# Rotary embedding over 16 heads: one input load in two parts, on two queues

## The chip, the cores and the metric

The kernel runs on one core of one Trainium2 chip. The metric is device time in microseconds, as the median of several runs of the whole program. A core has five instruction streams: TensorE (PE), VectorE (DVE), ScalarE (ACT), GpSimd (POOL) and SyncE (SP). Each runs its own instructions in order and waits on semaphores that the others, or finished transfers, count up. Transfers between HBM and the core's own memory (128 partitions) are done by 16 DMA engines; ScalarE and SyncE each have a queue on which they issue them.

## The reference

The input x has 16 batches of 512 rows of 1024 floats, seen as 16 heads of 64. Each head's two halves are rotated by tables of cosines and sines with one entry per row and half position.

```python
x = x.reshape(batch, seq, num_heads, head_dim)
x1, x2 = x[..., :half_dim], x[..., half_dim:]
cos = cos[None, :, None, :]
sin = sin[None, :, None, :]
rotated = np.concatenate([x1 * cos - x2 * sin, x1 * sin + x2 * cos], axis=-1)
```

Input and output are 33.55 MB each; the tables are 64 KB each.

## The kernel before

**Tiles.** The input is cut into 10 tiles: batches 0 and 1 alone, batches 2 to 13 in six pairs, batches 14 and 15 alone. In a single batch each partition holds 4 consecutive rows of x (16 KB), in a pair 8 rows (32 KB). So a single is a transfer of 2048 KB and a pair one of 4096 KB, and each is one DMA over 128 partitions. Tile 3, the second pair, is batches 4 and 5. The compute engines work on "rows": one row is 128 partitions by 1024 values, four of them in a single and eight in a pair, 64 rows (`u` from 0 to 63) in all. Tile 3 is rows 16 to 23.

**Memory.** `x_sb` is a ring of 40 rows, so it holds ten batches, tiles 0 to 5. The result of a row is written in place, and the tile is stored from there. Tiles 6 to 9 go into places that an earlier tile leaves, and can only be loaded when that one's store has landed.

**One row.** POOL (line 257) multiplies the row with its halves swapped by the sine table and writes `t2_sb` (6 buffers). VectorE (line 293) multiplies the row by the cosine table and writes `t1_ps` (3 buffers). The sum of the two is made in one of two ways: VectorE adds them (line 304), or, for three of eight rows in the middle (`PE2`), TensorE adds `t2` onto `t1` by a matmul with the identity (line 224) and ScalarE copies the sum out (line 191). One row of eight in each pair (`V2`) has its sine product done by VectorE too (line 286), not by POOL. `wait_added(eng, u)` waits until all rows up to u have been summed.

**Queues.** Loads are issued by ScalarE, stores by SyncE. `on_scalar` first issues the loads of tiles 0 to 5 in order (lines 166 to 168), with the two tables behind tile 0 (line 174). Later tiles are loaded from within its loop over rows (lines 188 to 195): at rows 17, 25 and 33 it waits for the landing of the stores that free the place (line 194) and issues tile 6, tile 7, and tiles 8 and 9. The wait of row 17 is for both single tiles' stores, those of rows 25 and 33 are for the stores of tiles 2 and 3. What ScalarE has to copy after that row stands behind this wait. `on_sync` (line 155) goes through the tiles in order, waits until all rows of a tile are summed and issues its store; the first one waits for rows 0 to 3.

**Landing.** Each tile has one semaphore `sem_in[t]`, counted up by 16 when its load has landed. POOL (line 255) and VectorE (line 279) wait for it at the first row of a tile.

Of the kernel before, what the change touches and what calls it, by code (L numbers as in the profile page):

```python
# [6 lines left out]
def bass_split_heads_rope_kernel(  # L7
# [20 lines left out]
    P = 128  # L28
    R1 = seq // P
# [38 lines left out]
    with ExitStack() as stack:  # L68
# [11 lines left out]
        sem_in = [stack.enter_context(nc.semaphore(f"in{t}")) for t in range(NT)]  # L80
# [20 lines left out]
        def c_of(t, r):  # L101
            return c1_ps[:, r, :] if tiles[t][1] == R1 else pair_ps[:, r // R1, 0, r % R1, :]

        def s_of(t, r):
            return s1_sb[:, r] if tiles[t][1] == R1 else s2_sb[:, r]

        x1 = x.rearrange("b (s r) d -> b s (r d)", r=R1)
        o1 = out.rearrange("b (s r) h d -> b s (r h d)", r=R1)
        x2 = x.rearrange("b s d -> (b s) d").rearrange("(g p r) d -> g p (r d)", p=P, r=R2)
# [3 lines left out]
        def in_dram(single, pairs, t):  # L113
            b, n = tiles[t]
            return single[b] if n == R1 else pairs[b // 2]

        def in_sbuf(t):
            b, n = tiles[t]
            k = b * R1 % RING
            return x_sb[:, k:k + n].rearrange("p n h t d -> p (n h t d)")  # L120

        def where(u):
            t, r = rows[u]
            return t, r, u % RING

        def swapped(k):
            return x_sb[:, k, :, ::-1, :]

        def over_heads(table):
            return table[:, None, :, :].broadcast_to([P, H, 2, HALF])  # L130

        def wait_added(eng, u):

            if n_pe[u]:
                eng.wait_ge(sem_a, n_pe[u])
            if n_comb[u]:
                eng.wait_ge(sem_v, n_comb[u])

        def wait_t2_free(eng, u):

            if u >= NT2:
                v = u - NT2
                if PE2[v]:
                    eng.wait_ge(sem_e, n_pe[v])
                else:
                    eng.wait_ge(sem_v, n_comb[v])

        def stores_of(k):

            return sum(b * R1 // R2 == k for b, _ in tiles)  # L150

        def load(eng, t):
            eng.dma_start(in_sbuf(t), in_dram(x1, x2, t)).then_inc(sem_in[t], 16)  # L153

        def on_sync(sp):
            for u in range(NU):
                t, r, k = where(u)
                if r == tiles[t][1] - 1:
                    wait_added(sp, u)
                    k = u // R2  # L160
                    sp.dma_start(in_dram(o1, o2, t), in_sbuf(t)).then_inc(sem_out[k] if k < EARLY else sem_rest, 16)
            sp.wait_ge(sem_rest, 16 * sum(stores_of(k) for k in range(EARLY, NU // R2)))

        def on_scalar(ae):
            later = {}
            for t, (b, n) in enumerate(tiles):
                if b * R1 + n <= RING:
                    load(ae, t)
                else:

                    later.setdefault((b * R1 - RING) // R2 * R2 + R2 - 1 + LAG, []).append(t)
                if t == 0:
                    for i, (table, sem) in enumerate(((cos, sem_cos), (sin, sem_sin))):
                        ae.dma_start(stage[:, i, :], table.rearrange("(s r) d -> s (r d)", r=R1)).then_inc(sem, 16)  # L174
# [13 lines left out]
            for u in range(NU):  # L188
                if PE2[u]:
                    ae.wait_ge(sem_e, n_pe[u])  # L190
                    ae.activation(xs[:, u % RING, :], t1_ps[:, u % NT1, :], COPY).then_inc(sem_a, 1)  # L191
                for t in later.get(u, ()):
                    k = (tiles[t][0] * R1 - RING) // R2
                    ae.wait_ge(sem_out[k], 16 * stores_of(k))
                    load(ae, t)
# [38 lines left out]
        def on_gpsimd(pl):  # L234
            pl.memset(ident[:], 1.0).then_inc(sem_i, 1)  # L235
            pl.wait_ge(sem_i, 1)
            pl.affine_select(  # L237
                out=ident[:],
                in_=ident[:],
                compare_op=mybir.AluOpType.is_equal,  # L240
                fill=0.0,
                base=0,
                pattern=[[-1, P]],
                channel_multiplier=1,
            ).then_inc(sem_i, 1)
            for u in range(NU):
                if V2[u]:
                    continue
                t, r, k = where(u)
                if (t, r) == (0, 0):  # L250
                    pl.wait_ge(sem_s, 1)
                if (t, r) == (2, 0):
                    pl.wait_ge(sem_s, 2)
                if r == 0:
                    pl.wait_ge(sem_in[t], 16)
                wait_t2_free(pl, u)
                pl.tensor_tensor(  # L257
                    t2_sb[:, u % NT2, :, :, :], swapped(k), over_heads(s_of(t, r)), mult
                ).then_inc(sem_p, 1)

        def on_vector(ve):
            ve.memset(zero[:], 0.0).then_inc(sem_z, 1)  # L262
            ve.wait_ge(sem_cos, 16)
            ve.tensor_copy(c1_ps, stage[:, 0, :].rearrange("s (r d) -> s r d", d=HALF)).then_inc(sem_c, 1)  # L264
            ve.wait_ge(sem_c, 1)
            ve.wait_ge(sem_w, NT1 * EH)

            def pair_tables():
                ve.wait_ge(sem_s, 2)
                row = pair_ps[:, V_ROW // R1, 1, V_ROW % R1, :]  # L270
                ve.tensor_scalar_mul(v_ps[:, 0, :], row, -1.0).then_inc(sem_c, 1)
                ve.tensor_copy(v_ps[:, 1, :], row).then_inc(sem_c, 1)

            first_v = V2.index(True)

            def mul(u):
                t, r, k = where(u)
                if r == 0:
                    ve.wait_ge(sem_in[t], 16)
                if (t, r) == (2, 0):  # L280
                    pair_tables()
                if u == first_v:
                    ve.wait_ge(sem_c, 3)
                if V2[u]:
                    wait_t2_free(ve, u)
                    ve.tensor_tensor(t2_sb[:, u % NT2, :, :, :], swapped(k), over_heads(v_ps), mult)  # L286
                if u >= NT1:
                    v = u - NT1
                    if PE2[v]:
                        ve.wait_ge(sem_a, n_pe[v])  # L290
                    else:
                        ve.wait_ge(sem_v, n_comb[v])
                ve.tensor_tensor(  # L293
                    t1_ps[:, u % NT1, :].rearrange("p (h d) -> p h d", d=HALF),
                    x_sb[:, k, :, :, :].rearrange("p h t d -> p (h t) d"),
                    c_of(t, r)[:, None, :].broadcast_to([P, 2 * H, HALF]),
                    mult,
                ).then_inc(sem_m, 1)

            def comb(u):  # L300
                t, r, k = where(u)
                ve.wait_ge(sem_m, u + 1)
                ve.wait_ge(sem_p, n_pool[u])  # L303
                ve.tensor_tensor(  # L304
                    xs[:, k, :],
                    t1_ps[:, u % NT1, :],
                    t2_sb[:, u % NT2, :, :, :].rearrange("p h t d -> p (h t d)"),
                    add,
                ).then_inc(sem_v, 1)

            for u in range(NU + LEAD):
                if u < NU:
                    mul(u)
                if u >= LEAD and not PE2[u - LEAD]:
                    comb(u - LEAD)

        on_sync(nc.sync)
        on_scalar(nc.scalar)
        on_gpsimd(nc.gpsimd)
        on_tensor(nc.tensor)  # L320
        on_vector(nc.vector)
# [33 lines left out]
```

## Time and profile before

| what | us |
|---|---|
| median of 3 timed runs (161.26 to 161.79) | 161.39 |
| span of the profiled execution, first to last instruction | 160.0 |
| POOL busy, 64 instructions | 134.9 |
| VectorE busy, 117 instructions | 130.1 |
| TensorE matmul busy | 73.7 |
| ScalarE busy | 24.4 |

The profile's times are those of one execution; "span" runs from its first instruction to its last, and the timed runs have some more around it. A group of instructions is named by its line in the kernel, engine and operation, with what it writes and reads. The transfers of the input issued from line 153, in order of issue:

| tile | issued at | lands after | landed at |
|---|---|---|---|
| 0 | 0.81 | 7.8 | 8.6 |
| 1 | 2.18 | 11.7 | 13.9 |
| 2 | 2.96 | 20.6 | 23.6 |
| 3 | 3.45 | 35.0 | 38.5 |
| 4 | 3.95 | 49.0 | 53.0 |
| 5 | 4.48 | 68.1 | 72.6 |
| 6 | 53.77 | 38.2 | 92.0 |
| 7 | 73.26 | 38.0 | 111.3 |
| 8 | 92.80 | 33.0 | 125.8 |
| 9 | 93.17 | 47.2 | 140.4 |

The stores of line 161:

| tile | issued at | lands after | landed at |
|---|---|---|---|
| 0 | 20.25 | 18.8 | 39.1 |
| 1 | 30.80 | 22.9 | 53.7 |
| 2 | 46.81 | 26.4 | 73.2 |
| 3 | 63.46 | 29.3 | 92.8 |
| 4 | 80.85 | 30.9 | 111.8 |
| 5 | 102.36 | 24.2 | 126.6 |
| 6 | 118.77 | 21.8 | 140.6 |
| 7 | 135.10 | 15.1 | 150.2 |
| 8 | 144.03 | 11.1 | 155.1 |
| 9 | 151.14 | 8.8 | 159.9 |

### The profile page before, as it was taken

What the parts mean: (1) busy time and instruction counts of PE and PEld (TensorE: products, weight loads), DVE (VectorE), ACT (ScalarE), POOL (GpSimd) and SP (SyncE); (2) the same over time, 40 slices, a digit from 0 to 9 for tenths busy, and PEclk for the clock granted to TensorE, in tenths of its full rate; (3) what the DMA queues carried; (4) which work ended last, traced back from release to release, by engine and by line L of the source; (5) the groups of instructions that cost most, each with busy time, mean ns of one, the idle gap of its engine ahead of it and who ended that gap; (6) DMA issues with size and microseconds to landing.
All of it is one profiled execution on the core that took longest, in us unless ns stands there. A gap on an engine that the chain in (4) does not pass through costs nothing.

```text
span 160.0 us, 522 instructions
## 1 busy us (share of the span) xinstructions
PE 73.7 (46%) x94; PEld 23.7 (15%) x94; DVE 130.1 (81%) x117; ACT 24.4 (15%) x27; POOL 134.9 (84%) x64
## 2 busy tenths in 40 slices
PE   6050005476427735690948606459439841970000
PEld 1020002021102220220222002002202210320000
DVE  0069998699999998997989709899999989989600
ACT  0420000205020502022022020220220122050000
POOL 1059999999999999999999999698999999289400
PEclk9999999969955865567555685855855599577555
DMA  5999999999999999999999999999999999999997
GB/s 160 401 451 463 401 430 418 410 483 406 401 463 406 494 401 401 483 426 401 467 426 418 410 467 434 401 467 393 420 463 446 418 414 418 479 410 434 414 414 303
DMA packets 3170, 67.26 MB, mean 420 GB/s; under 512 B 352, under 2 KB 608, under 8 KB 608
## 3 DMA queue, kind: packets, MB, share of 16 engines
q10 hardware_dynamic: 1728, 33.69, 49.7%
q1 hardware_dynamic: 1440, 33.56, 48.8%
q14 instruction: 2, 0.02, 0.0%
HBM read 33.69 MB, written 33.55 MB: 420 GB/s over the span
## 4 chain that ended last, share of the span: by engine, by line
DMA 59%; POOL 22%; PE 5%; DVE 3%; issue 2%; ACTq 1%; ACT 1%; DVEq 0%
DMA x_sb<-in_x_dram 41%; POOL t_sb L257 22%; DMA out_dram<-x_sb 18%; PE t_ps L224 5%; DVE x_sb L304 2%; DVE t_ps L293 1%; ACT x_sb L191 1%; ACTq L153 1%; ACTq L174 1%; DVEq L303 0%
## 5 line engine op out<-in xcount | busy, mean ns | idle before, releaser
L257 POOL TENSOR_TENSOR t_sb<-x_sb,s_sb 128x1024 f32<-128x1024 f32 x58 | 134.2, 2358 | 14.2 <-ACT s_sb L183 8.2
L224 PE MATMUL t_ps<-t_sb,ident 128*128 128x512 f32 x84 | 68.9, 973 | 62.8 <-DVE t_ps L293 37.9
L293 DVE TENSOR_TENSOR t_ps<-x_sb,pair_ps 128x1024 f32<-128x1024 f32 x48 | 57.7, 1223 | 9.7 <-ACT x_sb L191 9.7
L304 DVE TENSOR_TENSOR x_sb<-t_ps,t_sb 128x1024 f32<-128x1024 f32 x43 | 52.4, 1218 | 2.1 <-POOL t_sb L257 2.1
L191 ACT ACTIVATE x_sb<-t_ps 128x1024 f32<-128x1024 f32 x21 | 21.5, 1024 | 110.6 <-PE t_ps L224 98.9
L224 PEld LDWEIGHTS t_ps<-t_sb,ident 128*128 128x128 f32 x84 | 21.8, 286 | 109.6 <-DVE t_ps L293 70.0
L293 DVE TENSOR_TENSOR t_ps<-x_sb,tab_ps 128x1024 f32<-128x1024 f32 x16 | 19.3, 1222 | 0.5 <-ACT x_sb L191 0.5
L286 DVE TENSOR_TENSOR t_sb<-x_sb,tab_ps 128x1024 f32<-128x1024 f32 x6 | 7.3, 1212 | 0.0
L264 DVE COPY tab_ps<-stage 128x128 f32<-128x128 f32 x1 | 0.3, 295 | 7.7 <-DMA stage<-in_cos_dram 7.7
L208 PE MATMUL pair_ps<-stage,pick 128*128 128x256 f32 x4 | 2.0, 667 | 5.1 <-DMA stage<-in_sin_dram 5.1
L201 PE MATMUL t_ps<-zero 128*128 128x512 bf16 x6 | 2.7, 630 | 1.3 <-DVE zero L262 1.3
L208 PEld LDWEIGHTS pair_ps<-stage,pick 128*128 128x128 f32 x4 | 1.2, 324 | 6.2 <-issue 6.0
L177 ACT ACT_TABLE_LOAD x1 | 1.3, 1283 | 5.0 <-issue 5.0
L201 PEld LDWEIGHTS t_ps<-zero 128*128 128x128 bf16 x6 | 0.7, 138 | 2.3 <-DVE zero L262 1.2
L262 DVE MEMSET zero<- 128x256 uint32 x1 | 0.3, 272 | 0.9 <-PEq L337 0.9
L182 ACT ACTIVATE s_sb<-stage 128x128 f32<-128x128 f32 x1 | 0.3, 310 | 2.3 <-DMA stage<-in_sin_dram 2.3
L186 ACT ACTIVATE s_sb<-pair_ps 128x256 f32<-128x256 f32 x1 | 0.4, 384 | 1.7 <-PE pair_ps L208 1.7
L235 POOL MEMSET ident<- 128x128 f32 x1 | 0.2, 205 | 0.3 <-POOLq L337 0.3
L177 ACT ACTIVATE pick<-ident 128x256 f32<-128x256 f32 x1 | 0.4, 430 | 0.0
L187 ACT ACTIVATE s_sb<-pair_ps 128x256 f32<-128x256 f32 x1 | 0.4, 377 | 0.0
L237 POOL TENSOR_SCALAR_AFFINE_SELECT ident<-ident 128x128 f32<-128x128 f32 x1 | 0.3, 294 | 0.1
L337 POOL MEMSET const-float32-0.0<- 128x1 f32 x1 | 0.1, 99 | 0.3 <-issue 0.3
(6 smaller groups left out, 1.0 us busy)
## 6 DMA issues: line engine op xcount, KB each, us to landing
x_sb<-in_x_dram ACTq DMA_DIRECT2D x6, 4096.0 KB, 38.1
out_dram<-x_sb SPq DMA_DIRECT2D x6, 4096.0 KB, 25.3
x_sb<-in_x_dram ACTq DMA_DIRECT2D x4, 2048.0 KB, 22.4
out_dram<-x_sb SPq DMA_DIRECT2D x4, 2048.0 KB, 14.9
stage<-in_cos_dram ACTq DMA_DIRECT2D x1, 64.0 KB, 7.6
stage<-in_sin_dram ACTq DMA_DIRECT2D x1, 64.0 KB, 7.3
```

The lines of the kernel that those rows point to most:

```text
L153: eng.dma_start(in_sbuf(t), in_dram(x1, x2, t)).then_inc(sem_in[t], 16)
L174: ae.dma_start(stage[:, i, :], table.rearrange("(s r) d -> s (r d)", r=R1)).then_inc(sem, 16)
L177: ae.activation(pick[:], ident[:].rearrange("q (s k) -> q k s", k=2)[:, :, None, :].broadcast_to([P, 2, 2, P // 2]), COPY).then_inc(sem_g, 1)
L186: ae.activation(s2[:, :, :, 0, :], pair_ps[:, :, 1, :, :], COPY, scale=-1.0)
L191: ae.activation(xs[:, u % RING, :], t1_ps[:, u % NT1, :], COPY).then_inc(sem_a, 1)
L201: pe.matmul(t1_ps[:, k, b * BANK:(b + 1) * BANK], zero[:, 0:P], zero[:], start=True, stop=True).then_inc(sem_w, 1)
L208: pe.matmul(pair_ps[:, k].rearrange("p c r d -> p (c r d)"), pick[:, k].rearrange("q b s -> q (b s)"), stage[:].rearrange("q c f -> q (c f)"),
L224: ins = pe.matmul(t1_ps[:, u % NT1, b * BANK:(b + 1) * BANK], ident[:], t2[:, b * BANK:(b + 1) * BANK], start=False, stop=True, skip_group ...
L257: pl.tensor_tensor(t2_sb[:, u % NT2, :, :, :], swapped(k), over_heads(s_of(t, r)), mult).then_inc(sem_p, 1)
L286: ve.tensor_tensor(t2_sb[:, u % NT2, :, :, :], swapped(k), over_heads(v_ps), mult)
L293: ve.tensor_tensor(t1_ps[:, u % NT1, :].rearrange("p (h d) -> p h d", d=HALF), x_sb[:, k, :, :, :].rearrange("p h t d -> p (h t) d"), c_of ...
L304: ve.tensor_tensor(xs[:, k, :], t1_ps[:, u % NT1, :], t2_sb[:, u % NT2, :, :, :].rearrange("p h t d -> p (h t d)"), add,).then_inc(sem_v, 1)
```

## The change

Tile 3 is loaded by two DMAs instead of one. ScalarE issues, at the same place in its order as before, the part for partitions 0 to 95 (3072 KB). SyncE issues the part for partitions 96 to 127 (1024 KB) at the start of its work: it waits until rows 0 to 2 are summed, issues that part, and then goes on to the first store, which waits for rows 0 to 3 as before. Both parts count up the semaphore of tile 3, which is waited for at 32 instead of 16. All other loads, all stores and all compute instructions are as they were.

```diff
-        def load(eng, t):
-            eng.dma_start(in_sbuf(t), in_dram(x1, x2, t)).then_inc(sem_in[t], 16)
+
+        SHARED = 3
+        PART = P // 4
+
+        def load(eng, t, some=None):
+            if some is None:
+                some = slice(0, P - PART) if t == SHARED else slice(0, P)
+            eng.dma_start(in_sbuf(t)[some, :], in_dram(x1, x2, t)[some, :]).then_inc(sem_in[t], 16)
+
+        def wait_landed(eng, t):
+            eng.wait_ge(sem_in[t], 32 if t == SHARED else 16)
 
         def on_sync(sp):
+            wait_added(sp, R1 - 2)
+            load(sp, SHARED, slice(P - PART, P))
             for u in range(NU):
...
                 if r == 0:
-                    pl.wait_ge(sem_in[t], 16)
+                    wait_landed(pl, t)
...
                 if r == 0:
-                    ve.wait_ge(sem_in[t], 16)
+                    wait_landed(ve, t)
```

## The prediction

> **What bounds the kernel now.** The first view is the page's row of the DMA's busy share over 40 slices, with the queues below it (q10 carries what ScalarE's queue issues, all loads; q1 what SyncE's queue issues, all stores).
>
> ```profile
> span 160.0 us, 522 instructions
> DMA  5999999999999999999999999999999999999997
> q10 hardware_dynamic: 1728, 33.69, 49.7%
> q1 hardware_dynamic: 1440, 33.56, 48.8%
> HBM read 33.69 MB, written 33.55 MB: 420 GB/s over the span
> ```
>
> The reader is to see that the 16 DMA engines are busy in every slice but the first and the last: 49.7 + 48.8 = 98.5% of 160.0 us, 157.6 us. 67.25 MB at the 432 GB/s of the stretch from 111 to 140 us (next fence) are 155.7 us. So a kernel with the same bytes can't get much shorter by another order of work, and anything that makes the DMA engines less effective lengthens it at once.
>
> The second view is the DMA view cut to three stretches: 28 to 38 us, 53 to 72 us and 111 to 140 us (packets, MB, share of 16 engines).
>
> ```profile
> DMA packets 204, 4.41 MB, mean 441 GB/s; under 512 B 27, under 2 KB 27, under 8 KB 27
> q10 hardware_dynamic: 107, 3.01, 70.2%
> q1 hardware_dynamic: 97, 1.39, 32.5%
> ...
> q1 hardware_dynamic: 143, 4.19, 51.4%
> q10 hardware_dynamic: 142, 4.16, 50.8%
> ...
> DMA packets 568, 12.54 MB, mean 432 GB/s; under 512 B 65, under 2 KB 65, under 8 KB 65
> ```
>
> The two queues take turns packet by packet: 142 against 143 packets when both move batch pairs (32 KB a partition), and twice the bytes for loads when a pair's load meets a single batch's store (16 KB a partition). Both queues always have work from 20.3 us until the last load lands at 140.4 us (93.17 + 47.21 in the chain below), and then stores alone fill the engines.
>
> The third view is the chain that ended last, its late part, and the fourth the waits of POOL.
>
> ```profile
> 63.46 29.31 DMA out_dram<-x_sb
> 92.80 0.33 ACTq L153
> 93.17 47.21 DMA x_sb<-in_x_dram
> 140.45 9.30 POOL t_sb L257 x4
> 149.84 1.23 DVE x_sb L304
> ```
>
> ```profile
> POOL t_sb L257 <- DMA x_sb<-in_x_dram: 4.3, 2, 3.6
> POOL t_sb L257 <- PE t_ps L224: 1.6, 1, 1.6
> ```
>
> The chain is a store, a load that had to wait for it, and the last batch's work. POOL, the busiest engine (134.9 us), has 4.3 us of waits for loads in hand late in the run. The second to last store is issued at 144.03 us and lands 11.1 us later, at 155.1; the last is issued at 151.14. So about 4 us of stores are still to be moved when it arrives, and the end is the engines' end, not POOL's.
>
> **The change, part by part.** The sum is made against the profiled span, 160.0 us; the median shown, 161.39 us, stands 1.39 us above it, and I add that at the end.
>
> *Issue.* ScalarE's queue issues the load of tile 3 as before, one instruction (0.46 to 0.50 us for its neighbours), with 96 partitions instead of 128: no change. SP gains one wait and one DMA. The wait is for row 2's sum, the VectorE row that starts at 16.69 and takes 1.23 us, so it ends at 17.9 us; row 3's sum ends at 19.00 + 1.23 = 20.2 and releases the first store at 20.25. SP stands idle in between and one issue costs 0.33 to 0.37 us. Behind SP's new wait are only the stores, none ready before 20.2. Cost 0. The two waits for tile 3's semaphore (on POOL and VectorE) only count to 32 instead of 16. Cost 0, covered as below.
>
> *Order on the queues.* 1.05 MB leaves q10 and goes ahead of the first store on q1. All stores are pushed back, all loads from tile 3's main part on are pulled forward, the bytes remain. When both queues move pairs, SP's part takes turns with ScalarE's load, 216 GB/s each (the 53 to 72 us stretch halved), so it needs 4.85 us. It is issued 2.3 us before the store, so the first store starts about 2.5 us later, up to 4.5 with the term below. The store's landing is what ScalarE waits for before it loads a later tile (53.70, 73.2 and 92.8 us), and behind that wait stand its own copies. At 92.80 that wait already costs ScalarE 8.2 us of idle and POOL 1.6. So 2.5 to 4.5 us go on top there, and POOL has 4.3 us of later waits for loads to lose first. If that cover is gone, each further us delays the last store, which still has about 2 us to spare (its 4 us less some 2 us from issue to first data, by the first store: issued at 20.25, first bytes of q1 counted in the stretch from 22 to 24 us). The loads keep full queues: tile 6 is issued at 53.77 but its turn only comes when tile 5 lands at 72.6, 18.8 us of cover; tiles 7 and 8 have 18.7 and 18.5. Cost 0.
>
> *Landing of tiles 2 and 3.* Tile 2 now shares the engines with SP's part before it lands (23.6 us), so it comes 1.2 to 2.4 us later; VectorE needs it at 26.09, POOL at 28.4 (its ninth row: 9.62 + 8 x 2.35). Tile 3 landed at 38.45 and POOL needs it at about 45 (its sixteenth row, 9.62 + 15 x 2.35). Cost 0.
>
> *The narrow transfers themselves.* This is the term the trace doesn't show: every transfer of x in it covers all 128 partitions, 432 GB/s, 27 GB/s for each sixteenth. What a transfer into 32 or 96 partitions gets is bounded from two sides. At best the rate doesn't depend on partitions: 0. Nothing excludes a small gain, but the engines have none to give beyond the idle 0.3 us worked out below. At worst it falls with the share of partitions: 32 partitions at 108 GB/s are 9.7 us instead of 2.4 alone, +7.3 us; 96 at 324 GB/s are 9.7 instead of 7.3, +2.4 us. For the 32 I take the geometric middle, 216 GB/s, the rate into half of the partitions. SP's part would just use that up in its 4.85 us, but the load beside it brings another 1.05 MB at the same time, a half of it (tile 2) or a third (tile 3's main part) into the same half: 0.52 or 0.35 MB at 216 GB/s, 2.4 or 1.6 us. I take 2.0. For the 96: they run beside the first store, where loads got 3.01 MB in 10 us, 301 GB/s, which is below even 324, so on the average it costs nothing; but 301 of 324 leaves little room for engines that meet on the same partitions, so I take 0.4, near the lower end. As all 16 engines are full to the end, what they lose here is not won back.
>
> Sum: 160.0 + 0 + 0 + 2.0 + 0.4 = 162.4 us, and with 1.39 us around it **163.8 us**.
>
> [...] That both queues share the engines is what the 142 against 143 packets show; that a narrow transfer is no faster no run here shows. [...]
>
> **The rivals.** *No cost (not slower).* The narrow transfers move at 27 GB/s an engine like all others, because each engine is as busy with 2 and 6 partitions as with 8, or because each keeps its own partitions. Then only the order changes, the engines stay full, and the time is as before, 161.4 us. For it: the shares stay at 0.93 to 1.07 whatever the mix of loads, stores and packet sizes. Against it: no packet here goes to fewer partitions. It decides if the loss is under 0.5 us. It can gain a little, as the loads end earlier and the last store is issued earlier:
>
> ```profile
> 148.00:150.00 2.00, 0.00 (x0) 0.00 (x0) 1.33 (x3) 0.00 (x0) 1.74 (x1) 0.50 0.86 369
> 150.00:152.00 2.00, 0.00 (x0) 0.00 (x0) 1.07 (x1) 0.00 (x0) 0.00 (x0) 0.50 1.07 459
> ```
>
> (engines, granted clock, DMA share, GB/s). The only dip late in the run is 369 instead of 432 GB/s for 2 us, 0.3 us: 161.1 us.
>
> *The last store comes too late.* If SP's part takes 9.7 us (a quarter of the engines' reach), the first store starts 7.3 us later, and ScalarE's waits at 53.8, 73.3 and 92.8 us with it. POOL's 4.3 us of waits and the tail's 2 us cover 6.3; 1.0 us is left, in which the engines are dry at the end: 162.4 us with no other loss. It decides from 6.3 us of delay on. For it: the 8.2 us that ScalarE already stands at 92.80; against it: it needs three waits to pass on their delay whole.
>
> *Worst case of the forecast.* Both transfers at the proportional end: 7.3 + 2.4 = 9.7 us, 171.1 us. Against it: 96 partitions would need 9.7 us alone, and have some 10 us beside the store anyway.
>
> **How the numbers follow.** Slowed narrow transfers: 0.58, with 162.0 to 167.0 us as its own range and 0.09 of chance above that. No cost: 0.36. Late last store: 0.06. A measurement of this kernel can tell about 0.3%, 0.5 us (its three runs lie 0.53 us apart). Of the no-cost case I give 0.29 to within 0.3%, 0.07 to faster, since its gain is bounded at 0.3 us; the rest, 0.64, is slower. The range goes from 161.0, which takes in the no-cost case, to 167.0; some 0.05 lies below, 0.09 above. The time is that of the likeliest case.
>
> **What would show it.** Right: q1's first packets near 20 to 22 us instead of 22 to 24, total bytes equal; a GB/s row that drops under 400 for some 5 us from about 20 us on while the DMA share stays full (packets that take longer); the first store landing 2 to 5 us after 39.05; POOL's wait at 99.7 us grown to 4 to 6 us, and its waits for loads at 111 and 140 shrunk; the last landing some 2.4 us later. Wrong: a GB/s row as before at 20 to 40 us (then no cost), or a gap in the DMA row after 148 us (then the late store), or a loss much above 5 us in that stretch.

## The result and the profile after

The changed kernel takes 168.53 us (six runs, 167.73 to 170.0) against 161.37 us before: 1.0445 times as long, 95% interval 1.0419 to 1.0472. The forecast was slower, 163.8 us, with a range to 167.0; the direction held, the size did not. The kernel before and some of the others have single runs that are several us longer (before: 165.3 and 167.4 us beside 161.4); the ratios are formed without them.

Rows of the changed kernel's page: the share of time that the 16 DMA engines are busy (in tenths) and their rate over 40 slices, and the queues (packets, MB, share of 16 engines):

```profile
span 166.3 us, 523 instructions
DMA  5999999899999999999999999999999999999997
GB/s 169 412 432 445 465 252 252 260 311 378 394 414 453 441 431 449 426 410 449 418 449 426 449 426 449 418 410 441 441 443 410 433 449 418 441 418 465 386 441 299
q1 hardware_dynamic: 1488, 34.60, 50.1%
q10 hardware_dynamic: 1696, 32.64, 48.5%
```

The engines are as busy as before in every slice, to the end. But from the sixth slice to the eleventh (about 21 to 46 us) they move 252 to 394 GB/s, where before they moved 401 to 483. The same in stretches of 4 us of the changed kernel (after the granted clock: DMA share and GB/s):

```profile
20.00:24.00 4.00, 0.00 (x0) 0.00 (x0) 4.00 (x5) 0.00 (x0) 4.00 (x3) 1.00 1.19 352
24.00:28.00 4.00, 2.12 (x3) 1.12 (x4) 1.89 (x2) 0.00 (x0) 4.00 (x2) 1.00 1.01 229
28.00:32.00 4.00, 1.63 (x2) 0.06 (x1) 2.33 (x4) 1.02 (x1) 2.26 (x2) 1.00 0.91 258
32.00:36.00 4.00, 1.42 (x2) 0.83 (x3) 4.00 (x5) 0.00 (x0) 4.00 (x3) 0.61 0.90 274
36.00:40.00 4.00, 4.00 (x6) 1.39 (x5) 3.58 (x4) 1.02 (x1) 4.00 (x3) 0.53 1.06 352
40.00:44.00 4.00, 0.82 (x2) 0.00 (x0) 4.00 (x5) 1.02 (x1) 4.00 (x3) 0.89 1.00 401
```

Before, the six stretches had 430, 418, 410, 483, 406 and 401 GB/s, for example:

```profile
24.00:28.00 4.00, 2.03 (x3) 1.03 (x4) 3.31 (x5) 0.00 (x0) 4.00 (x2) 1.00 1.01 418
32.00:36.00 4.00, 3.11 (x4) 0.98 (x4) 4.00 (x5) 0.00 (x0) 4.00 (x3) 0.64 1.12 483
```

Over these 24 us the changed kernel moves 2.73 MB less; at 432 GB/s that is 6.3 us, and the span grew by 166.3 - 160.0 = 6.3 us. So all of this run's loss stands in the stretch in which tile 3 is loaded, and none of it is won back. (The profiled run is the shortest of the six. The medians lie 7.2 us apart, so 0.9 us more is lost in a typical run, and no view here shows where.) From 20 to 28 us, where SyncE's part runs, 1.07 MB are missing (2.5 us); from 28 to 44, where ScalarE's part runs, 1.66 MB (3.8 us).

The single packets say why. In the DMA view, packets and their share are counted by their start. From 21.3 to 22 us only packets of SyncE's part start:

```profile
q1 hardware_dynamic: 15, 0.49, 299.7%
```

299.7% of 16 engines for 0.7 us are 33.6 us for 15 packets of 32 KB: 2.24 us each. Before, packets of the same size from 16 to 20 us took 1.21 us each (92.9% of 16 x 4 us for 49):

```profile
q10 hardware_dynamic: 49, 1.61, 92.9%
```

The engine is busy for nearly twice as long with the same bytes. The packets of tile 2, whose load covers all 128 partitions, are slowed as well where they fall among them; from 23.3 to 24.4 us 15 of them took 1.78 us each:

```profile
q10 hardware_dynamic: 15, 0.49, 151.6%
```

The late chain and POOL's waits of the changed kernel:

```profile
32.31 31.14 DMA out_dram<-x_sb
63.47 0.34 ACTq L159
...
71.06 31.07 DMA out_dram<-x_sb
102.16 0.34 ACTq L159
```

```profile
POOL t_sb L268 <- PE t_ps L235: 7.8, 3, 3.7
POOL t_sb L268 <- DMA x_sb<-in_x_dram: 0.4, 1, 0.4
```

The stores of the early tiles land later (the first at 20.17 + 28.8 = 49.0 instead of 39.1 us), ScalarE issues tile 6 at 63.47 instead of 53.77, and its copies behind this wait and the two later ones now cost POOL 7.8 us instead of 1.6. POOL's waits for loads have shrunk from 4.3 to 0.4 us. As the engines stay full to the end, this shift by itself should cost this kernel nothing; an experiment below bears on that.

### The profile page after: what moved, and what is told of

It reads as the page before. It is cut to its first block, busy times and chain, and to the rows that moved or that the text cites. A ratio compares the mean times of both kernels' runs of the same rounds, so it can differ in the third digit from the quotient of the medians.

```text
span 166.3 us, 523 instructions
## 1 busy us (share of the span) xinstructions
PE 74.8 (45%) x94; PEld 24.4 (15%) x94; DVE 130.1 (78%) x117; ACT 24.4 (15%) x27; POOL 134.9 (81%) x64
## 4 chain that ended last, share of the span: by engine, by line
DMA 54%; DVE 16%; PE 11%; issue 7%; ACT 4%; ACTq 2%; DVEq 0%; SPq 0%
DMA out_dram<-x_sb 37%; DMA x_sb<-in_x_dram 16%; PE t_ps L235 11%; DVE t_ps L304 8%; DVE x_sb L315 7%; ACT x_sb L202 4%; DVE t_sb L297 1%; ACTq L159 1%; ACTq L185 1%; DVE tab_ps L283 0%; DVE tab_ps L282 0%; DVEq L301 0%; DVEq L314 0%; SPq L137 0%
## 5 line engine op out<-in xcount | busy, mean ns | idle before, releaser
L235 PE MATMUL t_ps<-t_sb,ident 128*128 128x512 f32 x84 | 70.0, 987 | 68.9 <-DVE t_ps L304 46.3
L235 PEld LDWEIGHTS t_ps<-t_sb,ident 128*128 128x128 f32 x84 | 22.5, 295 | 116.3 <-DVE t_ps L304 74.7
L202 ACT ACTIVATE x_sb<-t_ps 128x1024 f32<-128x1024 f32 x21 | 21.5, 1024 | 117.8 <-PE t_ps L235 95.2
```

Of the source, the lines that this page charges most:

```text
L235: ins = pe.matmul(t1_ps[:, u % NT1, b * BANK:(b + 1) * BANK], ident[:], t2[:, b * BANK:(b + 1) * BANK], start=False, stop=True, skip_group ...
```

## The experiments

Three theories were put against each other: *paths* (a contiguous block of partitions uses only some of the ways into the core's memory), *narrowness* (few partitions per engine are slow, whichever they are) and *order* (a load on SyncE's queue ahead of the first store is what costs). The "ways" are a guess of mine and no more than a picture: no view shows them. What the runs can show is whether it matters which partitions a transfer covers.

**The same split over all partitions.**

```diff
+        CUT = 6 * H * HD
...
-                some = slice(0, P - PART) if t == SHARED else slice(0, P)
-            eng.dma_start(in_sbuf(t)[some, :], in_dram(x1, x2, t)[some, :]).then_inc(sem_in[t], 16)
+                some = slice(0, CUT) if t == SHARED else slice(None)
+            eng.dma_start(in_sbuf(t)[:, some], in_dram(x1, x2, t)[:, some]).then_inc(sem_in[t], 16)
...
-            load(sp, SHARED, slice(P - PART, P))
+            load(sp, SHARED, slice(CUT, None))
```

`CUT` is six rows, 6 x 1024 values, of each partition; ScalarE's part is these six rows of all 128 partitions, SyncE's the other two.

> Three theories stand. Paths: a transfer into a contiguous block of 32 or 96 partitions loads some of the ways into the core's memory more than others, while its 16 engines all wait for them. Narrowness: an engine works slower whenever it is given few partitions, whichever they are. Order: the loss comes from a load that runs on SyncE's queue ahead of the first store, beside ScalarE's load. Here the same bytes go to the same queues at the same places in the order, but both parts cover 128 partitions (six rows of each partition on ScalarE's queue, two on SyncE's). Paths and narrowness: 161.4 us, within 0.5, as before the change. Order: 168 us or close to it.

162.99 us, 1.0102 of before (1.0061 to 1.0143). Order as the main cause falls: the same bytes on the same queues in the same order lose 1%, not 4.4%. But a loss of nothing, as paths had it, is wrong too. The rate holds while tile 3 is loaded (428 GB/s from 20 to 28 us, 439 from 28 to 44); the loss stands elsewhere. Late stretches and POOL's wait of this kernel:

```profile
136.00:140.00 4.00, 3.78 (x4) 1.18 (x4) 4.00 (x4) 0.16 (x1) 4.00 (x3) 0.50 0.68 295
140.00:144.00 4.00, 1.82 (x2) 0.84 (x3) 3.59 (x4) 0.86 (x1) 4.00 (x3) 0.50 0.62 262
```

```profile
POOL t_sb L270 <- PE t_ps L237: 7.2, 3, 3.7
```

Here the DMA engines run dry, 0.68 and 0.62 busy, while POOL and VectorE are still at work on rows whose stores are not yet ready. Tile 6 is issued at 60.39 instead of 53.77 us, since the early stores were pushed back by 6.6 us; POOL has lost 7.2 us to ScalarE's held-up copies. This is the prediction's rival of the late last store, without the slow packets that hide it in the change.

**The same, with ScalarE's waits three rows later.** `LAG` sets the row of ScalarE's loop at which it waits for an early store; with 13 these are rows 20, 28 and 36 instead of 17, 25 and 33.

```diff
-    LAG = 10
+    LAG = 13
```

> The split over 128 partitions again (rows 0 to 5 and 6 to 7), with one number changed: ScalarE waits for the early stores three rows later in its loop (LAG 13 instead of 10), so that fewer of its copies stand behind these waits. If the 1% that the split alone cost comes from the stores' later landing, which holds up ScalarE's copies, then POOL, until the last stores are issued too late: 161.2 us, no loss left. If it comes from the second queue's transfer itself: 163 us as without it.

161.7 us, 1.0018 (1.0005 to 1.0030). POOL no longer waits for the held-up copies at all, and the second queue's transfer, if it covers all partitions, is all but free. So the 1% was the wait, not the transfer; that the kernel before gains nothing from the same edit is shown below.

**The changed kernel with the same LAG.**

> The changed kernel with LAG 13 instead of 10. If its loss lies in the transfers' own time, as the packets of the trace say, it stays at 168 to 169 us, whatever ScalarE waits for. If the held-up copies are part of it: 166 to 167 us.

169.96 us, 1.0515 (1.0442 to 1.0587). Longer than the 168 to 169 us expected, and not faster than the change (1.0445; the two intervals overlap). POOL's 7.8 us of wait for the copies are gone, its waits for loads have grown from 0.4 to 10.7 us. So the held-up copies are no part of the change's loss.

**The kernel before with the same LAG.**

> The kernel before with LAG 13 instead of 10, nothing else. POOL's wait for the held-up copies (1.6 us) should go, but the DMA engines are full to the end, so the time stays: 161.3 us, within 0.4. If POOL's waits set the end: some 160 us.

161.36 us, 1.0001 (0.9983 to 1.0019): POOL's 1.6 us of wait for the copies were gone, its waits for loads grew from 4.3 to 5.9 us, and the time stayed. Before the change, too, the DMA engines alone set the end.

**Both narrow parts on ScalarE's queue.**

```diff
+                    if t == SHARED:
+                        load(ae, t, slice(P - PART, P))
...
-            wait_added(sp, R1 - 2)
-            load(sp, SHARED, slice(P - PART, P))
```

> The same two narrow parts, but both on ScalarE's queue, one behind the other in the place of the one load; SyncE issues only stores. Paths and narrowness: still slower, 164 to 168 us, as both narrow parts remain; paths expects less than 168.5, since the part of 32 partitions now runs beside a store instead of beside another load. Order: 161.4 us.

167.35 us, 1.0397 (1.0352 to 1.0443). Without any load on SyncE's queue most of the loss remains. From 20 to 44 us this kernel moves 324 GB/s instead of 425, 5.6 us at 432 GB/s; its span is 5.4 us longer than before. The loss follows the narrow parts, not the queue.

**Four quarters, contiguous or strided.** Tile 3 in four transfers of 32 partitions, three on ScalarE's queue and the fourth on SyncE's. The two kernels differ in one line:

```diff
-            return slice(i * PART, (i + 1) * PART)
+            return slice(i, P, 4)
```

> Four quarters as in the strided case, with the same number of transfers, sizes and queues, but contiguous: partitions 0 to 31, 32 to 63 and 64 to 95 on ScalarE's queue, 96 to 127 on SyncE's. Paths: as slow as the change or slower, 168 to 172 us, since each quarter loads one part of the ways. Narrowness: the same as the strided case. Order: about 168 us.

> The four quarters of the tile are now every fourth partition (0, 4, 8 ... then 1, 5, 9 ... and so on), each a transfer of 32 partitions: three on ScalarE's queue, the fourth on SyncE's queue ahead of the first store. Every transfer is as narrow as SyncE's part in the change, but reaches over all 128 partitions. Paths: 161.4 us, within 0.5. Narrowness: 168.5 us or more, as all four transfers are narrow now, up to 172. Order: about 168 us.

Contiguous: 171.22 us, 1.0619 (1.0595 to 1.0643). From 20 to 48 us this kernel moves

```profile
20.00:48.00 28.00, 11.68 (x16) 3.95 (x16) 22.18 (x22) 3.07 (x3) 24.32 (x11) 0.85 1.01 284
```

284 GB/s at a full DMA share. The strided one, from 20 to 44 us, and its SyncE part from 21.5 to 23 us:

```profile
20.00:44.00 24.00, 10.94 (x15) 3.85 (x16) 21.93 (x22) 3.07 (x3) 24.00 (x11) 0.91 1.01 425
```

```profile
q1 hardware_dynamic: 16, 0.52, 80.9%
```

425 GB/s, as before the change (424.7 on the average of its six stretches), and 80.9% of 16 x 1.5 us for 16 packets, 1.21 us each. Both kernels issue transfers of 32 packets of 32 KB; only which partitions they cover, and with them which rows of the input, differs. So narrowness falls. Of paths, what is shown is that it matters which partitions are covered: 284 against 425 GB/s.

The strided kernel's whole time doesn't show this: two of its runs took 162.7 and 163.1 us and two 167.4 and 168.3, and none is within 0.5 of 161.4 us, as paths had expected. Four more runs of the same kernel:

> The strided quarters once more, on another call, since its first runs lay apart by 5.6 us. Paths: the runs near 163 us show its cost, 162.5 to 163.5 us, as of the split over 128 partitions, and the longer ones come from one DMA engine that falls behind late in the run. Narrowness: no run under 165 us.

165.5 to 169.1 us; the expectation of runs near 163 us was missed. The profiled one of these runs loses nothing at 20 to 44 us but late:

```profile
20.00:44.00 24.00, 12.17 (x14) 4.36 (x15) 21.78 (x22) 3.07 (x3) 24.00 (x11) 0.57 1.00 423
...
156.00:167.00 11.00, 0.00 (x0) 0.00 (x0) 1.77 (x2) 0.00 (x0) 1.52 (x1) 0.50 0.54 229
```

423 GB/s while tile 3 is loaded, and 0.54 of the engines' time in use in the last 11 us (0.31 from 155 to 160 us): it looks as if some engines were late and the others had nothing left. Why is open; the profiled one of the first four ends in the same way. That narrowness is not the cause rests on the packets and the rate, not on the kernel's time.

**The transfers alone.** At the start, each issued only when the one before has landed: 32 partitions, 96 partitions, then tile 0. The kernel's whole time, 181.6 us, includes this waiting and is not compared.

```diff
+            ae.wait_ge(sem_in[SHARED], 16)
+            load(ae, SHARED)
+            ae.wait_ge(sem_in[SHARED], 32)
+            load(ae, 0)
+            ae.wait_ge(sem_in[0], 16)
...
-            wait_added(sp, R1 - 2)
```

> A measurement of the disputed cost by itself: before anything else is moved, the part of partitions 96 to 127 (1024 KB), then the part of partitions 0 to 95 (3072 KB), then tile 0 (2048 KB over 128 partitions) are loaded, each issued when the one before has landed; the rest follows as in the changed kernel, so its whole time has no meaning beyond some 20 us more. Paths: 32 partitions take as long from issue to landing as tile 0 with twice the bytes (4.85 us at 216 GB/s, about 7 us with what lies around a transfer), and 96 partitions take 9.7 us plus the same 2 us. If a narrow transfer alone runs at 432 GB/s: 2.4 and 7.3 us plus 2 us.

The issues (KB, us to landing) and the queue from 14 to 22 us, when only the 96 partitions are loaded, and from 25 to 33 us, when tile 0 and the two tables are:

```profile
x_sb<-in_x_dram ACTq DMA_DIRECT2D x1, 3072.0 KB, 16.8
x_sb<-in_x_dram SPq DMA_DIRECT2D x1, 1024.0 KB, 7.3
```

```profile
q10 hardware_dynamic: 54, 1.77, 100.6%
...
q10 hardware_dynamic: 144, 2.10, 72.3%
```

Tile 0, 2048 KB over 128 partitions, landed after 7.6 us; its 128 packets of 16 KB took 0.72 us each. 32 partitions need nearly the same time for half the bytes, as paths expected. The 96 missed its expectation of about 11.7 us: 16.8. Its 54 packets in 8 us are 221 GB/s, 2.38 us a packet. From 10 to 14 us it is 26 packets in 96.8% of 16 x 4 us, 2.38 us again, so the transfer doesn't consist of a slow part and a fast one. So a contiguous block of 96 partitions is loaded at half rate just as one of 32 is, not at three quarters.

**Halves.**

```diff
-        PART = P // 4
+        PART = P // 2
```

> The tile is split in halves: partitions 0 to 63 on ScalarE's queue, 64 to 127 on SyncE's. Paths: SyncE's half costs some 3 us while it runs beside tile 2, nothing while it runs beside the other half, which needs the other ways, and ScalarE's half some 1 to 2 us more beside the first store: 165 to 167 us, less than the change although more bytes are in SyncE's part. Narrowness, with 4 partitions for each engine instead of 2 and 6: no clear number, at most as slow as the change.

172.38 us, 1.0706 (1.0642 to 1.0771), well above the 165 to 167 expected. The stretch in which both halves run, and the DMA view of two moments in it, 29 to 31 and 31.3 to 33.2 us:

```profile
22.00:40.00 18.00, 8.78 (x10) 3.21 (x11) 13.72 (x15) 2.05 (x2) 16.18 (x8) 0.82 1.06 231
```

```profile
q1 hardware_dynamic: 16, 0.52, 116.1%
q10 hardware_dynamic: 1, 0.00, 0.1%
...
q10 hardware_dynamic: 16, 0.52, 122.1%
```

I had expected the two halves not to hinder each other. The rate says otherwise: 16 packets of the one queue start (2.32 us each), then 16 of the other, and 231 GB/s is the result. But the turns overlap. From 32.3 to 33.2 us ten packets of ScalarE's half start, 2.32 us each, so they run to 34.6 us and beyond; from 33.6 to 34.5 us six of SyncE's half start:

```profile
q10 hardware_dynamic: 10, 0.33, 161.0%
...
q1 hardware_dynamic: 6, 0.20, 96.6%
```

So for a time both halves are being loaded, and the packets are no faster. Why two halves don't add up is open: it is 231 GB/s for two against 221 for one narrow transfer alone.

One rival can be set aside here. A contiguous block of partitions is also one contiguous piece of the input, so it could be the source that is slow. But each half is 2 MB in one piece, and so is tile 0 above: over 128 partitions it needed 0.72 us for 16 KB, the halves 2.32 us for 32 KB.

**A store in two parts.** Loads as before; the store of tile 4 is issued as partitions 0 to 95 and 96 to 127.

```diff
-                    sp.dma_start(in_dram(o1, o2, t), in_sbuf(t))...
+                    for some in (slice(0, 96), slice(96, P)) if t == 4 else (slice(0, P),):
+                        sp.dma_start(in_dram(o1, o2, t)[some, :], in_sbuf(t)[some, :])...
```

> The kernel before, with all loads as they were; only the store of tile 4 (the third pair) is issued in two parts, partitions 0 to 95 and 96 to 127, one behind the other on SyncE's queue. If the ways are as narrow for reading as for writing: both parts lose as in the one-queue case, 164 to 168 us. If they bind writes alone: 161.2 us.

166.5 us, 1.0347 (1.0270 to 1.0424). While the two parts are stored, and at the end:

```profile
88.00:116.00 28.00, 14.49 (x18) 3.86 (x16) 22.31 (x20) 4.10 (x4) 23.95 (x12) 0.68 1.00 388
...
160.00:164.60 4.60, 0.00 (x0) 0.00 (x0) 0.00 (x0) 0.00 (x0) 0.00 (x0) 0.50 0.34 146
```

From 108.9 to 112 us, near the end of this store, the packets of SyncE's queue were

```profile
q1 hardware_dynamic: 27, 0.79, 102.4%
```

that is 24 packets of 32 KB at 2.1 us each, and three small ones. So reading a contiguous block of partitions is slow too, at least in that stretch. 388 instead of 432 GB/s for 28 us are 2.9 us; the rest of the span's 4.6 us is at the end, where a third of the engines' time is still in use: the loss seems to have fallen on some engines more than on others.

## Why the prediction was wrong in its size

**What bounds the kernel** was right. The DMA engines are full from 20 us to the end in the changed kernel too, and the loss in the packets (6.3 us) is the loss in the span (6.3 us).

**Issue and the waits for landing** cost nothing, as said. Tile 2 came late, at 2.75 + 26.9 = 29.7 instead of 23.6 us, 6 us rather than the 1.2 to 2.4 of the prediction; VectorE waited 3.8 us for it, POOL 1.7. That cover, priced at nothing, did break, but the engines behind it were full.

**The order on the queues** was put at 0 for the change, and with the slow packets that holds, though the stores were put off by 9.7 us (tile 6's issue) and not by 2.5 to 4.5. Its price shows where packets are fast: in the wide split the early stores landed 6.6 us later, and the time rose by 1.6 us. The rival of the late last store had named this place and this mechanism. It was to decide from 6.3 us of delay on and gave 1.0 us for 7.3, so 0.3 for 6.6; its cover was sized too high.

**The narrow transfers themselves** is the step that failed, above all by its second term. For the 32 partitions I took 2.0 us, an estimate that rests on 216 GB/s into a half of the partitions; no run shows that rate as a limit of a half. What the runs showed: from 20 to 28 us 2.5 us were lost, alone these partitions landed after 7.3 us where a tile of twice their bytes took 7.6, and two halves together got 231 GB/s. In its size the term was about right. For the 96 partitions I took 0.4 us; from 28 to 44 us 3.8 us were lost. Its lower bound, 324 GB/s, came from letting the rate fall with the share of partitions; measured alone it is 221 GB/s, so my bound was no bound, and the demand of 301 GB/s that I held to be below it was far above. With 221 GB/s, 3.15 MB alone need 14.2 us instead of 7.3, 6.9 us more. Beside the first store, 3.8 us is what was measured. So the GB/s row stayed under 400 for some 20 us, not for the 5 us that I named as the sign of being right.

Every fourth partition at 1.21 us a packet stands against 2.47 us for the contiguous quarter on SyncE's queue (32 packets in 61.7% of 16 x 8 us, from 20 to 28 us). Why 96 contiguous partitions, 2.38 us a packet alone, are as slow as 32 stays open: no run shows the reason.

**The no-cost rival** (0.36) fell for contiguous blocks and holds for a split over all partitions: 1.0018 once ScalarE's waits are out of the way. What spoke for it, a busy share of 0.93 to 1.07 whatever the mix, was no evidence: the share reached 1.12 from 32 to 36 us before the change, and in the change it was 0.90 to 1.19 from 20 to 44 us while the rate fell to as little as 229 GB/s, where it had been 418.

## What to carry to other kernels

If the DMA engines are full, look at how each transfer lies on the partitions before its size or queue: 32 KB packets of a load over a contiguous block of 32, 64 or 96 partitions took 2.2 to 2.5 us here (221 to 231 GB/s with little else under way), those of a store in such parts up to 2.1 us in the stretches shown, and those of a load over all 128, or over every fourth partition, 1.21 us. To give a queue a part of a tile, cut along the free dimension and keep all partitions: so split, this kernel took 1.0102 of the time before, and 1.0018 with ScalarE's waits three rows later, against 1.0445. And before putting anything ahead of a store, find who waits for that store and what stands behind that wait: 6.6 us of delay was enough to let the engines run dry (0.68 and 0.62 busy) at the far end of the kernel.

## What was not expected of the hardware

A block of 96 partitions was as slow as one of 32 (221 GB/s; 2.38 us a packet alone, against 2.24 for the 32 in the change). Two transfers to opposite halves on two queues were hardly faster than one narrow transfer alone (231 against 221 GB/s). The DMA engines' busy share didn't show it: from 20 to 44 us of the change it was 0.90 to 1.19, while the rate fell to as little as 229 GB/s.
